# Convolved tiles of the Mamba layer made in half-product pairs ahead of the scans, and two products' rows loaded in place

## The chip, the cores and the metric

The kernel runs on one core of one Trainium2 chip. The metric is device time in microseconds (us) of one execution; lower is better. The median of three runs of the kernel before is 1600.65 us (1600.18 to 1603.64). A measurement of this kernel can tell a difference of about 0.2%, which is 3.2 us.

## The reference, cut to what matters

One step of a two-layer decoder on 1024 new prompt tokens and 8 x 8 sample tokens (1088 token columns in all), in float32. The first layer is a Mamba-2 layer, the second a pooling layer. Of the first layer only this matters here:

```python
zxbcdt = h @ w_in                                   # h: 1088 x 1024
z   = zxbcdt[..., :D_INNER]                         # 16 tiles of 128 channels, the gate
xbc = zxbcdt[..., D_INNER:D_INNER + CONV_DIM]       # 32 tiles: B, C (8 each), x (16)
conv = conv_b + sum(xp[:, k:k + L] * conv_w[k] for k in range(4))
xbc_act = jax.nn.silu(conv)
y, new_ssm = ssd_scan(xs, dt, A, Bm, Cm, ssm_prev)  # 8 groups, chunks of 128 tokens
gated = (y + d_skip * xs) * silu(z)                 # then an RMS norm per group
out = gated @ w_out
```

Group g has four convolved tiles, numbered (g, 0) for B, (g, 1) for C, and (g, 2), (g, 3) for x, and two gate tiles, 2g and 2g + 1. The last three columns of each convolved tile before the convolution are an output too (`ncT`).

## The kernel before, in words

Activations lie with channels on the 128 partitions and the 1088 tokens along the free axis. A float32 product is made of three matmuls per 128x128 weight block (high by high, high by low, low by high part).

**Two ways to make a projection tile.** The direct way (`mm3`, line 205) takes 8 blocks of the contraction x 3 chunks of 364, 364 and 360 columns x 3 matmuls = 72 matmuls; a chunk of 24 is called a unit. The half-product way (`fast_pair`, with `product` and `w_sums`) makes two tiles at once by seven half-size products instead of eight: 7 products x 2 chunks of 272 columns x 4 blocks x 3 = 168 matmuls. Its operands are sums of halves of the activations, which stand ready during the front stage, and sums of halves of the weights, which GpSimd makes; ScalarE and VectorE (and GpSimd for 2 of 7) split them.

**The front** (`front_pairs`, line 1470) makes eight such pairs, listed in `FRONT`: the twelve gate tiles 4 to 15 (stored to memory after their silu) and the four convolved tiles of group 0. `after` is called at named points within a pair and does the silus, the stores and the convolution (`proj_end`, line 388).

**The scans** (`scan`, line 1577, for groups 0 to 7, four parts p each) follow. Between a scan's small TensorE steps the order written out by hand puts units of a filler (`fills`, line 1517): `PACE[g][p]` = (a, b, c) says how many units come before `scan_front`, before `scan_y` and after it. The filler gives first the four direct tiles of each of groups 1 to 7 (`proj_group`, line 412), 12 units a group, then product 2 and product 6 of the output projection. In the scans the order on TensorE is pinned; a scheduler orders the other engines. `silu_burst` (line 397) does the silu of the next group's four tiles. VectorE convolves (`conv_tile`, line 356), scales and masks for the scan (lines 551 to 568), adds states (586, 702) and evacuates (593). The stream of weight tiles (`stream_next`) goes through three buffers `wr`, loaded by the SyncE queue (SP), with the adaLN weights of `ADA` between them.

**The output projection** also works by half-products: seven products, in the order 2, 6, 5, 3, 1, 4, 7. Each needs eight blocks `b` made of halves of the sixteen gated rows `gyd` (`block_steps`, line 1074): ScalarE copies the high part (line 1100) and VectorE subtracts (1101), after a sum or difference (1099) where two halves enter. For product 2 rows 0 to 7 are loaded whole into slots of their own (`load_row`, line 1647), kept, and used again for product 6; six of them are dropped then and loaded again for product 3. Line 1195 splits the output weights, line 1219 adds a product to the residual. `gate_last` (line 748) finishes the rows of group 7, which product 5 needs. Slots are 30 buffers of 1088 columns handed out in the order they came free.

## Time and profile before

| what | value |
|---|---|
| median of 3 runs | 1600.65 us |
| the profiled execution, its own time | 1602.45 us |
| its span in the profile | 1600.7 us |
| granted TensorE clock, mean over the span | 0.993 |
| front pairs | about 93 to 266 us |
| scans beside their filler | about 266 to 845 us |
| rest of the output projection, layer 2 | from 845 us |

The span is 1.75 us shorter than the execution's own time. A window's row gives its length, then the busy time of each engine in it, then the granted clock as a share, the busy share of the DMA engines and GB/s. Matmuls overlap, so their own durations add up to more than the time; the start-to-start distance, a stretch divided by its count, is what one costs. A wait's row says which engine and line sat idle, what ended the wait, the sum, the count and the longest.

### The profile page before, as it was taken

Reading aid. Unit: us, or ns where it says so; the run is one execution under the profiler, and the core shown is the slowest. Engines: PE = TensorE matmul, PEld = TensorE weight load, DVE = VectorE, ACT = ScalarE, POOL = GpSimd, SP = SyncE. Lnnn points to the kernel's source line nnn. Section 1 sums busy time; section 2 is a strip of 40 time slices with the busy share of each in tenths; the row PEclk is TensorE's granted clock in tenths of the full one; section 3 lists DMA queues with packets and bytes.
Section 4 is the critical chain, followed back from the end, with each engine's and each line's share of the span. In section 5 each row is a group of like instructions: output and inputs, shape, how many; then the busy total and the mean of one; then the engine's idle time right before and its main releaser. Section 6 shows DMA issues by size and latency. Waiting matters only on the chain.

```text
span 1600.7 us, 31079 instructions
## 1 busy us (share of the span) xinstructions
PE 1571.2 (98%) x12399; PEld 1514.0 (95%) x12399; DVE 1259.6 (79%) x2019; ACT 807.3 (50%) x1432; POOL 453.0 (28%) x484
## 2 busy tenths in 40 slices
PE   8999999999999999999999999999999999999997
PEld 6899999999999999999889999999999999999997
DVE  6975477888778878877987989788889777667886
ACT  6663344676666666566742468423333243333354
POOL 0133451212122122212020022765666530000231
PEclk9999999999999999999999999999999999999999
DMA  9422326866474655647779662233333379565773
GB/s 352 167 97 71 109 83 221 296 205 225 161 239 150 212 170 180 208 142 257 259 233 306 174 163 84 73 129 102 116 114 114 105 253 357 143 179 166 174 168 113
DMA packets 110730, 282.99 MB, mean 177 GB/s; under 512 B 18268, under 2 KB 42232, under 8 KB 110584
## 3 DMA queue, kind: packets, MB, share of 16 engines
q1 hardware_dynamic: 102520, 257.52, 47.0%
q0 software_dynamic: 5760, 19.01, 6.8%
q10 hardware_dynamic: 2304, 4.46, 0.7%
q8 instruction: 98, 1.61, 0.4%
q14 instruction: 48, 0.39, 0.1%
HBM read 214.59 MB, written 64.13 MB: 174 GB/s over the span
## 4 chain that ended last, share of the span: by engine, by line
PE 83%; issue 4%; DMA 4%; DVE 4%; ACT 2%; POOL 1%; SPq 0%; DVEq 0%; ACTq 0%; POOLq 0%
PE mm L101 29%; PE st L101 28%; PE op L101 13%; PE y L101 3%; PE S L101 2%; PE pl L101 2%; PE am L101 2%; PE tr L104 1%; PE tr L101 1%; DMA row<-gyd 1%; PE ms L101 1%; PE p L101 1%; DMA wr<-win 1%; DVE b L1101 1%; DMA acb<-acd 1%
## 5 line engine op out<-in xcount | busy, mean ns | idle before, releaser
L101 PE MATMUL op<-b,w 128*128 128x272 f32 x2688 | 347.0, 290 | 6.5 <-DVE w L1195 4.8
L101 PEld LDWEIGHTS op<-b,w 128*128 128x128 f32 x2688 | 341.1, 190 | 11.2 <-DVE w L1195 5.6
L101 PE MATMUL st<-hh,w 128*128 128x272 f32 x1408 | 273.9, 289 | 0.0
L101 PE MATMUL mm<-hh,wh 128*128 128x364 f32 x720 | 246.2, 342 | 0.0
L101 PE MATMUL mm<-hl,wh 128*128 128x364 f32 x720 | 236.4, 328 | 0.0
L101 PE MATMUL mm<-hh,wl 128*128 128x364 f32 x720 | 236.4, 328 | 0.0
L101 PEld LDWEIGHTS st<-hh,w 128*128 128x128 f32 x1408 | 223.9, 188 | 0.3 <-issue 0.3
L101 PE MATMUL st<-t,w 128*128 128x272 f32 x1584 | 205.6, 288 | 1.4 <-POOL w L195 1.4
L101 PE MATMUL st<-hl,w 128*128 128x272 f32 x704 | 202.8, 288 | 0.0
L101 PEld LDWEIGHTS st<-t,w 128*128 128x128 f32 x1584 | 201.1, 188 | 1.6 <-POOL w L195 1.6
L101 PEld LDWEIGHTS mm<-hh,wh 128*128 128x128 f32 x720 | 135.4, 188 | 13.5 <-issue 9.7
L193 ACT ACTIVATE w<-wr 128x512 fp32r<-128x512 f32 x88 | 55.6, 632 | 169.5 <-PE st L101 137.6
L101 PEld LDWEIGHTS mm<-hl,wh 128*128 128x128 f32 x720 | 135.4, 188 | 0.7
L101 PEld LDWEIGHTS mm<-hh,wl 128*128 128x128 f32 x720 | 135.3, 188 | 0.0
L101 PEld LDWEIGHTS st<-hl,w 128*128 128x128 f32 x704 | 132.6, 188 | 0.0
L585 POOL TENSOR_TENSOR hd<-h,cd 128x256 f32<-128x256 f32 x56 | 70.7, 1262 | 131.1 <-DVE h L586 52.4
L369 POOL COPY ncv<-raw 128x3 f32<-128x3 f32 x32 | 18.1, 564 | 287.3 <-ACT raw L439 275.7
L364 DVE SCALAR_TENSOR_TENSOR raw<-raw,vec,raw 128x1112 f32<-128x1112 f32 x64 | 90.2, 1409 | 9.8 <-ACT raw L362 9.4
L195 POOL TENSOR_TENSOR w<-wr,w 128x512 fp32r<-128x512 f32 x44 | 79.9, 1816 | 46.2 <-ACT w L193 45.9
L1219 DVE SCALAR_TENSOR_TENSOR x<-op,gat,x 128x272 f32<-128x272 f32 (+1 forms) x160 | 72.8, 477 | 25.5 <-PE op L101 23.0
L957 DVE TENSOR_TENSOR u<-st,u 128x272 f32<-128x272 f32 (+1 forms) x158 | 61.2, 408 | 38.8 <-PE st L101 36.8
L195 DVE TENSOR_TENSOR w<-sw,w 128x512 fp32r<-128x512 f32 x66 | 65.9, 998 | 26.3 <-ACT w L193 26.2
(277 smaller groups left out, 3205.1 us busy)
## 6 DMA issues: line engine op xcount, KB each, us to landing
wr<-win SPq DMA_DIRECT2D x48, 512.0 KB, 4.2
acb<-acd SPq DMA_DIRECT2D x32, 512.0 KB, 4.5
wr<-pin SPq DMA_DIRECT2D x32, 512.0 KB, 3.5
wr<-pout SPq DMA_DIRECT2D x28, 512.0 KB, 5.3
wr<-wout SPq DMA_DIRECT2D x20, 512.0 KB, 5.3
wr<-pout POOLq DMA_DIRECT2D x20, 512.0 KB, 5.8
row<-gyd SPq DMA_DIRECT2D x18, 544.0 KB, 7.8
x<-xT SPq DMA_DIRECT2D x16, 544.0 KB, 7.6
```

What stands on the lines that cost most here:

```text
L101: return self.pin(self.build.nc.tensor.matmul(*a, **k))
L104: return self.pin(self.build.nc.tensor.transpose(*a, **k))
L193: self.nc.scalar.activation(hi, src, AF.Copy)
L195: eng.tensor_tensor(out=lo, in0=src, in1=hi.bitcast(F32), op=ALU.subtract)
L364: nc.vector.scalar_tensor_tensor(out=acc[:, :n], in0=raw[:, k:k + n], scalar=w[k], in1=acc[:, :n], op0=ALU.mult, op1=ALU.add)
L369: nc.gpsimd.tensor_copy(ncv[:, 0:1, :], raw[:, 1024:1027].unsqueeze(1))
L585: nc.gpsimd.tensor_tensor(out=hd, in0=h, in1=cd[:, :, cc].unsqueeze(2).to_broadcast([P, 4, 64]), op=ALU.mult)
L957: nc.vector.tensor_tensor(out=out, in0=x, in1=y, op=ALU.add)
L1101: nc.vector.tensor_tensor(out=t[:, HALF:], in0=s, in1=t[:, :HALF].bitcast(F32), op=ALU.subtract)
L1219: ins = nc.vector.scalar_tensor_tensor(out=x[e][:, a:a + pn], in0=ps[:, :pn], scalar=g, in1=x[e][:, a:a + pn], op0=ALU.mult, op1=ALU.add)
```

## The change: what it does, and the diff

Eight convolved tiles, `MOVED`: (1, 1) to (7, 1) and (7, 2), are made in the front. The front has twelve pairs: each moved tile with one gate tile, the four tiles of group 0 in two pairs, and two pairs of gate tiles. A moved tile is convolved, gets its silu and is stored to memory (`xbd`); the filler loads it where it would have made it. The filler has 9 units for each of groups 1 to 6, and `PACE` is cut to match. The three columns for `ncT` are stored by tile in the front and by run of kept tiles in the scans. For products 2 and 6 of the output projection a new `row_blocks` loads the rows (the first half for 2, the whole for 6) straight into the block's own buffer and splits there; rows 0 to 7 are not kept, and all eight are loaded for product 3.

```diff
-PACE = (((0, 1, 2), (0, 1, 2), (0, 1, 2), (0, 1, 2)),) * 6 + (((0, 1, 2), (0, 1, 2), (0, 3, 5), (0, 0, 4)), ((0, 1, 1), (0, 1, 2), (0, 1, 0), (0, 1, 1)))
+PACE = (((0, 1, 1), (0, 1, 1), (0, 1, 1), (0, 1, 2)),) * 6 + (((0, 2, 2), (0, 2, 2), (0, 1, 2), (0, 1, 2)), ((0, 1, 1), (0, 1, 2), (0, 1, 0), (0, 1, 1)))
-FRONT = (("z", 2), ("z", 3), ("z", 4), ("z", 5), ("b", 0), ("z", 6), ("x", 0), ("z", 7))
+MOVED = tuple((g, 1) for g in range(1, 8)) + ((7, 2),)
+FRONT = ((4, 5), ((1, 1), 6), ((2, 1), 7), ((3, 1), 8), ((0, 0), (0, 1)), ((4, 1), 9), ((5, 1), 10), ((0, 2), (0, 3)), ((6, 1), 11), ((7, 1), 12), ((7, 2), 13),
+         (14, 15))
...
     def proj_end(self, G, ii, raw, ahead=False):
         dst = self.slots.get("xbc")
         self.conv_tile(G["ti"][ii], raw, dst, G["ncv"][:, ii])
+        g, nt = G["g"], self.io["ncT"][G["g"]]
         if ahead:
             self.nc.scalar.activation(dst, dst, AF.Silu)
+            self.nc.sync.dma_start(nt[:, ii], G["ncv"][:, ii])
+            if (g, ii) in MOVED:
+                self.nc.sync.dma_start(self.xbd[g, ii], dst)
+                self.slots.free(dst)
+                return
...
         for ii in range(4):
+            if (G["g"], ii) in MOVED:
+                dst = self.slots.get("xbc")
+                nc.sync.dma_start(dst, self.xbd[G["g"], ii])
+                G["out"].append(dst)
+                continue
             w = self.stream_next()
...
+    def row_blocks(self, m, lag):
+
+        nc, sl = self.nc, self.slots
+        out, raw = [], []
+        self.blocks[m] = out
+        while len(out) < 8:
+            k = len(raw)
+            if k < 8 and (sl.a[self.reserve:] or sl.b):
+                t = sl.get("b", F32R)
+                raw.append(t)
+                nc.sync.dma_start(t[:, HALF * (m == 2):].bitcast(F32), self.gyd[k][:, :HALF * (1 + (m == 6))])
+            if k >= min(len(out) + lag, 8):
+                t = raw[len(out)]
+                hi, x = t[:, :HALF], t[:, HALF:].bitcast(F32)
+                if m == 6:
+                    s = self.stage(len(out))
+                    nc.vector.tensor_tensor(out=s, in0=hi.bitcast(F32), in1=x, op=ALU.add)
+                    x = s
+                nc.scalar.activation(hi, x, AF.Copy)
+                nc.vector.tensor_tensor(out=t[:, HALF:], in0=x, in1=hi.bitcast(F32), op=ALU.subtract)
+                out.append(t)
             yield
...
         first = []
         for n, pair in enumerate(FRONT):
             outs, ends = [], []
             for i in pair:
                 if isinstance(i, tuple):
                     G = self.proj_open(i[0])
...
-        yield from itertools.islice(pr, 9)
+        yield from itertools.islice(pr, 9 - 3 * len([i for i in MOVED if i[0] == 7]))
...
-        blk = self.block_steps(2, self.rows, False, 3, self.load_row)
+        blk = self.row_blocks(2, 3)
...
-        yield from self.out_units(2, self.block_steps(6, self.rows, drop=6))
+        yield from self.out_units(2, self.row_blocks(6, 2))
```

## Rows read from the trace of the kernel before

**Rows 1.** The page: span, and busy time of each engine (share, instructions).

```profile
span 1600.7 us, 31079 instructions
PE 1571.2 (98%) x12399; PEld 1514.0 (95%) x12399; DVE 1259.6 (79%) x2019; ACT 807.3 (50%) x1432; POOL 453.0 (28%) x484
```

**Rows 2.** The chain that ended last: start, length, what, matmuls.

```profile
69.63 22.17 PE mm L101 x132
...
154.61 111.62 PE st L101 x891
...
1026.29 295.02 PE st L101 x2352
1321.31 95.62 PE mm L101 x576
```

**Rows 3.** Busy time by window: front pairs, group 0's period, group 3's period.

```profile
154.61:266.22 111.61, 111.61 (x892) 111.61 (x892) 70.78 (x125) 44.69 (x70) 43.44 (x43) 1.00 0.31 105
...
285.20:356.45 71.25, 70.40 (x574) 65.96 (x576) 56.69 (x83) 47.16 (x96) 13.99 (x25) 1.00 0.77 254
...
517.78:588.64 70.86, 70.86 (x587) 66.31 (x588) 57.32 (x79) 46.88 (x94) 14.27 (x25) 1.00 0.58 192
```

**Rows 4.** Waits of PE, first 110.43 to 266.22 us, then all of 266 to 740 us.

```profile
PE st L101 <- POOL w L195: 1.4, 1, 1.4
...
PE am L101 <- DMA wr<-adaG: 0.9, 1, 0.9
```

**Rows 5.** VectorE groups of a convolved tile, 517.78 to 588.64 us (four tiles).

```profile
L364 DVE SCALAR_TENSOR_TENSOR raw<-raw,vec,raw 128x1112 f32<-128x1112 f32 x8 | 11.2, 1401 | 0.8 <-ACT raw L362 0.8
...
L365 DVE SCALAR_TENSOR_TENSOR xbc<-raw,vec,raw 128x1024 f32<-128x1024 f32 x4 | 5.1, 1276 | 0.0
L159 DVE TENSOR_TENSOR wl<-wr,wh 128x1024 fp32r<-128x1024 f32 x4 | 4.9, 1223 | 1.3 <-ACT wh L158 1.3
...
L367 DVE SCALAR_TENSOR_TENSOR xbc<-raw,vec,raw 128x64 f32<-128x64 f32 x4 | 1.5, 367 | 0.0
```

**Rows 6.** Waits in the SP queue: 95 to 266 us, then 266 to 740 us.

```profile
SPq L450 <- ACT z L814: 45.5, 10, 11.9
...
SPq L525 <- ACT cd L566: 91.5, 25, 11.0
```

**Rows 7.** Transfers issued from 517.78 to 588.64 us: count, size, median us to landing.

```profile
acb<-acd SPq DMA_DIRECT2D x4, 512.0 KB, 5.3
...
z<-zsd SPq DMA_DIRECT2D x2, 544.0 KB, 7.1
```

**Rows 8.** Busy time by window, scans of groups 6 and 7 and what follows.

```profile
700.00:860.00 160.00, 152.59 (x1303) 142.07 (x1301) 131.74 (x220) 93.47 (x191) 27.77 (x35) 0.99 0.74 246
...
760.00:820.00 60.00, 54.97 (x508) 50.01 (x507) 57.02 (x103) 39.71 (x85) 8.80 (x10) 0.97 0.84 282
800.00:820.00 20.00, 16.37 (x149) 13.94 (x148) 18.73 (x33) 10.85 (x27) 6.00 (x4) 0.91 0.95 330
840.00:860.00 20.00, 17.93 (x145) 17.70 (x143) 11.48 (x23) 4.86 (x8) 2.04 (x3) 1.00 1.03 332
860.00:880.00 20.00, 18.87 (x130) 18.87 (x131) 18.12 (x35) 7.50 (x10) 0.87 (x1) 0.83 0.82 284
```

**Rows 9.** Waits of PE from 740 to 862 us.

```profile
PE op L101 <- DVE w L1195: 3.2, 1, 3.2
PE tr L104 <- DVE h L702: 2.5, 1, 2.5
```

**Rows 10.** VectorE around product 5's blocks and weights, in order of time.

```profile
842.29 2.62 DVE L1101 TENSOR_TENSOR b<-xbc,b 128x544 fp32r<-128x544 f32 x4
...
859.22 0.72 DVE L1099 TENSOR_TENSOR bs<-row,row 128x544 f32<-128x544 f32 x1 [6.37 <-DMA row<-gyd]
859.86 1.22 DVE L1195 TENSOR_TENSOR w<-wr,w 128x1024 fp32r<-128x1024 f32 x1
```

**Rows 11.** The chain from 825 to 845 us: last units of the scans.

```profile
831.78 3.67 PE ms L101 x16
835.45 3.05 PE op L101 x24
```

More of the change, by code (lines that the diff above doesn't have):

```diff
@@ L1072, in op_begin, with block_steps @@
         self.nc.vector.tensor_scalar(self.ngat, self.gat[l][:, :, 8], -1.0, None, op0=ALU.mult)
-    def block_steps(self, m, rows, alt=False, lag=0, load=None, drop=0, ahead=0):
+    def block_steps(self, m, rows, alt=False, load=None):
         nc, sl = self.nc, self.slots
@@ L1086, in block_steps @@
             yield
-        for i in range(lag):
-            load(i)
-            yield
         for k in range(8):
-            if load and k + lag + ahead < 8:
-                load(k + lag + ahead)
+            if load and k < 6:
+                load(k + 2)
             while not (sl.a[self.reserve:] or sl.b) or any(rows[k + 8 * o[0]] is None for o in opnds):
@@ L1301, in run @@
         items += [(io["win"][i], 8) for i in (4, 5, 10, 11)]
-        items += [(io["win"][6 * g + {"b": 0, "x": 2, "z": 4}[kind] + i], 0) for kind, g in FRONT for i in range(2)]
-        todo = [(3 * t, [(io["win"][6 * (1 + t // 4) + t % 4], 8)]) for t in range(28)]
-        todo += [(LEAD + 12 * g + (1, 4, 7, 10)[p] - 0.5, self.ada_items(a)) for (g, p), a in self.ada_plan.items()]
+        items += [(io["win"][6 * i[0] + i[1] if isinstance(i, tuple) else 6 * (i // 2) + 4 + i % 2], 0) for pair in FRONT for i in pair]
+        left = [(g, ii) for g in range(1, 8) for ii in range(4) if (g, ii) not in MOVED]
+        todo = [(3 * t, [(io["win"][6 * g + ii], 8)]) for t, (g, ii) in enumerate(left)]
+        done = lambda g, p: LEAD + sum(sum(PACE[i // 4][i % 4]) for i in range(4 * g + p)) + sum(PACE[g][p][:2])
+        todo += [(done(g, p) - 0.5, self.ada_items(a)) for (g, p), a in self.ada_plan.items()]
         for _, its in sorted(todo, key=lambda t: t[0]):
@@ new lines, in front_pairs @@
+        first = []
+        for n, pair in enumerate(FRONT):
+            outs, ends = [], []
+            for i in pair:
+                if isinstance(i, tuple):
+                    G = self.proj_open(i[0])
+                    if i[0] == 0:
+                        G["out"] = first
+                    t = self.proj_begin(G, i[1])
+                    outs.append((t, 3, t[:, 1027:1115].rearrange("p (b w) -> p b w", w=11)[:, :, 3:11]))
+                    ends.append(G)
+                else:
+                    t = sl.get("z")
+                    outs.append((t, 0, None))
+                    ends.append(None)
+            def after(x):
+                for i, at in enumerate((("B21", "B22"), ("z01", "z11"))):
+                    if x in at and not ends[i]:
+                        a = HALF * at.index(x)
+                        self.z_chunk(outs[i][0], outs[i][0][:, a:a + HALF], a, HALF)
+                    if x == ("B22", "T4")[i] and not ends[i]:
+                        self.gate_store(pair[i], outs[i][0])
+                    elif x == "B22" and ends[i]:
+                        self.proj_end(ends[i], pair[i][1], outs[i][0], True)
@@ L1514, in front_pairs @@
         self.scans = [SimpleNamespace(g=g, h=[None], M={}, acb={}) for g in range(8)]
-        self.scans[0].T = G["out"]
+        self.scans[0].T = first
     def fills(self):
@@ L1598, in scan @@
             self.units(fill, b)
-            if p == 3 and g < 6:
-                self.silu_burst(after.T)
+            if p == 3 and after:
+                self.silu_burst(after)
             self.scan_y(s, p, self.sample_y if p == 3 else None)
@@ L1630, in scan @@
             if p == 3 and after:
-                if g == 6:
-                    self.units(fill, c - 3)
-                    self.silu_burst(after.T[3:])
                 self.scan_front(after, 0)
@@ L1638, in scan @@
                     self.gate_rows(s)
-                self.units(fill, c - 1 if g < 6 else 2)
+                self.units(fill, c - 1)
             else:
@@ L1697, in load @@
                 self.load_row(k)
-        self.out_product(5, self.block_steps(3, rows, load=load, ahead=2))
+        self.out_product(5, self.block_steps(3, rows, load=load))
         self.out_product(3, self.block_steps(1, rows, True))
```

45 lines of the change are left out of this document (13 added, 32 removed).

## The prediction

> **What bounds the kernel now.** I read the page first: TensorE is busy for 98% of the span, and no other engine is above 79% [rows 1]. Matmuls overlap, so a high share alone proves little; the chain of waits comes next, and there long runs of matmuls follow one another with nothing between [rows 2]. So what counts is how many matmuls there are and how far apart they start, and then where TensorE waits. In the table of waits there is one in the front pairs (1.4 us, for a weight difference that GpSimd makes) and one in the scans up to 740 us (0.9 us, for an adaLN weight load in group 0) [rows 4]. In the steady scans TensorE is never idle, and VectorE is at 57.32 of 70.86 us, 81% [rows 3]. The stretch after that is different: from 700 to 860 us TensorE loses 160.00 - 152.59 = 7.4 us, most of it from 760 to 820 us, where VectorE is busy 57.02 of 60 us, 95% [rows 8]. Two waits stand out there, 3.2 us for output weights and 2.5 us for a sample state, both with VectorE [rows 9], and after each the granted clock drops: 0.91 and 0.83 of the windows at 800 and 860 us [rows 8], which is part of the time at 1.2 instead of 2.4 GHz.
>
> **The front gains.** A matmul of a pair starts every 111.62 / 891 = 125.3 ns; the pairs of layer 2 agree, 295.02 / 2352 = 125.4 ns. A direct one starts every 22.17 / 132 = 168.0 ns, in layer 2 every 95.62 / 576 = 166.0 ns [rows 2]. A pair costs 168 x 125.3 = 21.05 us, two direct tiles 2 x 72 x 167 = 24.05 us: 3.0 us less per pair (2.9 to 3.1 with either direct spacing). Sixteen tiles a front becomes twenty-four: four more pairs, 84.2 us, and eight direct tiles less, 96.2 us. Term 1: **-12.0 us** (-11.4 to -12.6), if nothing waits. A weighing of this term: the Trainium skill, "TensorE: Matmul & The Clock Gate", section "Back-to-back issue gap", gives for a matmul by itself the columns divided by 2.4 GHz plus 2.5 ns. That would be 115.8 and 154.2 ns here, and an estimate from it gains 2.7 us a pair and 10.7 us in all; the trace's spacings are longer, and I stay with them.
>
> **What feeds the front pairs.** Each of eight pairs now carries one convolution. By the rows of four tiles [rows 5], one costs VectorE 2 x 1.40 + 1.28 + 0.37 = 4.4 us. The old front has VectorE at 70.78 of 111.61 us with four convolutions, GpSimd at 43.44, ScalarE at 44.69 [rows 3]: 13.3 us of VectorE in each 21.05 us pair, 0.75 of a convolution included. One whole convolution a pair makes 14.5 us. So TensorE covers it, at 69%; without that cover a convolution would cost its 4.4 us. On SP a moved tile adds a state load, a store of three columns and a store of the tile, which waits for its silu; behind it stand the weight loads of the next pair. The same place already holds gate stores that wait up to 11.9 us for their silu [rows 6], and TensorE waited only the 1.4 us. I take 0 (0 to 1.4 per added pair, 5.6 in all); nothing here can go below 0.
>
> **The scans get less cover.** A period of a group, 70.86 us [rows 3], loses three units, 12.0 us, and becomes 58.8 us. VectorE loses one convolution and one weight split, 4.4 + 1.2 = 5.6 us by single durations [rows 5] (they overlap a little, so about 5.3 of busy time): 57.3 - 5.3 = 52.0 us of 58.8, 88%. ScalarE has the same loss of about 5 from 46.88: 41.9 us, 71%. Reading back a moved tile is one transfer of 544 KB, 7.1 us to landing for its like [rows 7]; it is issued at least one tile, some 12 us, before its scan begins, so it is hidden. The transposed copies and the masks of part p must be ready one unit sooner than before. The loads `acb` sit in one buffer, 5.3 us to landing [rows 7], and the SP queue waited 91.5 us in 25 times for ScalarE to give that buffer back [rows 6]; whatever stands behind, weights and moved tiles, waits with it.
>
> What these tighter scans cost TensorE no row shows. Bounds: 0, as at 81% [rows 4]; and what 760 to 820 us lost at 95%, 5.0 us of idleness and 0.09 x 20 = 1.8 us of clock, 6.8 of 60 us or 11% [rows 8], which would be 6.7 us a group. Below 0 is excluded, since these scans have no wait to lose but 0.9 us. The work is that of the 81% row, and the nearest crowding in it is group 0, whose transfers at 0.77 of the DMA engines gave one wait of 0.9 us [rows 3, 4]; with the same bytes in 58.8 us, group 3's 0.58 becomes 0.70. I take one such wait in each of six groups. Term 2: **+5.4 us** (0 to 40).
>
> **Groups 6 and 7.** Here two tiles go, 24.0 us of TensorE, counted in term 1. VectorE from 700 to 860 us has 131.74 us [rows 8] and loses 2 x 5.3: 121.1 us, which at the best sustained share of 95% needs 127.5 us. TensorE needs 160 - 7.4 - 1.8 - 24.0 = 126.8 us. The two are level, so the idleness of before (7.4 + 1.8 = 9.2 us) can shrink to 0.7, but the reason for it, VectorE at 95%, is not gone. In-place rows cost the engines nothing: the copy, the subtraction and the sum for each block are those of before. They cost transfers: eight half rows and two whole rows more, 8 x 272 + 2 x 544 KB = 3.3 MB, beside what moves at 246 GB/s with the DMA engines 0.74 busy [rows 8]. I take no change, 0 (-8.5 to +10, the latter 3.3 MB at the 332 GB/s of the fullest window).
>
> **The start of product 5.** The 3.2 us wait [rows 9] comes from VectorE: in its queue a sum of rows for product 3 waits 6.37 us for a row's landing, ahead of the weight split that TensorE needs [rows 10]. With the clock it costs 2.1 + 1.1 us of idleness and 0.17 x 20 = 3.4 us, 6.6 in all [rows 8]. Rows no longer held free slots, so these loads may come sooner; that speaks for a gain. Against it: the filler ends two units sooner, so after group 7's norm (831.78 + 3.67 us) only one unit of 3.05 us and a state product of some 1 us [rows 11] cover the blocks made from its rows, which were done at 842.29 + 2.62 = 844.9 us [rows 10]. Product 5 would ask for the first of them near 840.7 and be done with a chunk near 842.2, so a new wait of up to 2.8 us. Ends -6.6 and +2.8; neither row is nearer, so I take the middle. Term 3: **-2.0 us**.
>
> **Sum.** -12.0 + 5.4 + 0 - 2.0 = -8.6 us. The profiled execution took 1602.45 us, 1.75 more than its span and 1.8 more than the median, so it would become 1593.85, and the median 1600.65 - 8.6 = **1592.0 us**.
>
> **Rivals.**
> - The scans hold with no wait, and the late row goes: -12.0 - 6.6 = 1582 us, with groups 6 and 7 freed as well 1573.5. For it: not one wait for VectorE up to 740 us [rows 4]. Against it: 88% is new.
> - Given back: transfers of rows, 10 us on the path between 700 and 860 us, eat the front's gain, 1600.65 - 12.0 + 10 = 1598.7; or 2.0 us a group do, 1600.65. For it: 1.03 of the DMA engines at 840 us [rows 8].
> - Slower: the backlog of VectorE at the end of part 2 and in part 3 of each scan, where the sample steps and the gate's scaling meet the convolution. If the next step on TensorE waits as it does for a sample state between 800 and 820 us, 2.5 us and then 1.8 us of clock [rows 8, 9], six groups lose 26 us: 1600.65 - 12.0 + 26 = 1614.7. It decides from 12.0 / 6 = 2.0 us a group. For it: VectorE fills that stretch; against: the same stretch of each period has no wait of TensorE now [rows 4]. The rule that fits is in the Trainium skill, "TensorE: Matmul & The Clock Gate", section "HAM oscillation — how this bites in real kernels": gaps between bursts of matmuls put the engine back to the lower clock, at every gap anew. The trace agrees: 0.91 and 0.83 of the clock behind the two long waits [rows 8, 9].
> - The pairs do not gain: fed too slowly they cost the 24.05 us of two direct tiles, 1600.65 + 3. Eight old pairs speak against it.
>
> **How the numbers follow.** My forecast (some waits in the scans, 1585 to 1597) has 0.58, no waits 0.15, given back 0.12, slower 0.14, no gain in the pairs 0.01. Faster by over 0.2% is below 1597.4: 0.58 + 0.15 = 0.73. Within 0.2%: 0.13. Slower: 0.14. The range takes in the first rival down to 1577 and the second up to 1604; left out are the slower rival and the extreme of the first, under 0.2.
>
> **What would show it.** In the changed profile: twelve stretches of 168 half-product matmuls at 125 ns and an end of the front near 350 us; a period of group 1 to 5 near 59 us with VectorE near 88%; the rows of TensorE's waits inside the scans, few and under 1 us each; the granted clock at 1.00 until group 6; the wait before line 1195 gone or smaller, and one for a block at the start of product 5. A period of 61 us or more, or clock drops inside groups 1 to 5, would make the forecast wrong; so would pairs over 22 us.

## The result, and the profile after

The changed kernel takes **1622.07 us** (median of 4 runs, 1621.53 to 1626.24) where the kernel before, on the same chip, takes 1601.61: a ratio of **1.0132 [1.0112, 1.0153]**. The forecast was 1592.0 with a range up to 1604. The profiled execution took 1621.86 us.

The page and the chain of waits of the changed kernel, for [rows 1] and [rows 2]; lines in the file moved by 2 near the matmul helper (L103) and by some 35 in the later half.

```profile
span 1620.0 us, 31607 instructions
PE 1568.6 (97%) x12495; PEld 1508.3 (93%) x12495; DVE 1307.7 (81%) x2095; ACT 803.4 (50%) x1426; POOL 491.8 (30%) x508
```

```profile
153.32 185.69 PE st L103 x1482
```

TensorE is busy for 2.6 us less than before in a span that is 19.3 us longer: it waits. The front's stretch is exactly what was forecast, 185.69 / 1482 = 125.3 ns a matmul, with nothing in between. So the loss is behind it. Windows of the changed kernel (length; busy PE, weight load, VectorE, ScalarE, GpSimd; granted clock, DMA share, GB/s): the front, then the periods of groups 0, 1, 2 and 4, for [rows 3].

```profile
153.32:339.01 185.69, 185.69 (x1485) 185.69 (x1484) 147.64 (x222) 77.09 (x117) 98.48 (x97) 1.00 0.29 94
362.80:434.20 71.40, 61.20 (x503) 55.61 (x502) 54.25 (x81) 45.58 (x97) 10.88 (x21) 0.93 0.82 275
434.20:496.10 61.90, 60.84 (x535) 55.28 (x533) 51.75 (x77) 42.60 (x89) 10.95 (x21) 1.00 0.69 227
496.10:560.60 64.50, 61.08 (x515) 55.86 (x514) 52.72 (x76) 41.97 (x88) 12.65 (x21) 0.97 0.63 205
621.40:681.80 60.40, 59.43 (x514) 54.46 (x514) 50.51 (x74) 40.29 (x87) 10.94 (x21) 1.00 0.68 219
```

Group 0 takes 71.40 us, as long as before with three units more. Group 2 takes 64.5, group 4 60.4; 58.8 was forecast. Both lose to single waits. The four longest of TensorE's waits (total, times, longest), for [rows 4, 9]:

```profile
PE am L103 <- DMA wr<-adaG: 7.7, 1, 7.7
PE op L103 <- ACT w L1231: 7.1, 2, 6.3
PE tr L106 <- ACT xbc L412: 4.7, 3, 2.4
PE op L103 <- ACT raw L456: 3.6, 1, 3.6
```

**Group 0.** The chain of waits of the changed kernel, and below it what SP issued at that time (start, length, line):

```profile
375.86 5.25 DMA acb<-acd
...
381.14 1.06 ACT ea L575
382.20 2.35 ACT M L580 x8
...
385.75 4.58 DMA acb<-acd
```

```profile
375.86 0.39 SPq L542 DMA_DIRECT2D acb<-acd  x1
376.35 1.98 SPq L1183 DMA_DIRECT2D wpd<-wp  x2
378.43 3.54 SPq L1195 DMA_DIRECT2D wp<-wout  x4
385.75 0.38 SPq L542 DMA_DIRECT2D acb<-acd  x1
386.18 0.50 SPq L141 DMA_DIRECT2D wr<-adaG  x1
```

One buffer holds `acb`: the next load waits until ScalarE has read the last, so a load, an exponential (L575), nine activations on `M` (L580, L581) and a small one follow one another, 9.9 us a turn (375.86 to 385.75). SP stands until 385.75 for that buffer, and the second adaLN weight tile of part 1 stands behind it in its queue and is issued at 386.18. TensorE wanted it at 383.9 and got on at 391.7; 2.1 us more went to the weights behind it. With TensorE idle for 10.2 of the 71.40 us, some 2 us of the loss are left for the lower clock (an estimate: 12.1 us lost less 10.2). The Trainium skill, "DMA: Bandwidth & Descriptors", section "Anatomy of one DMA — SWDGE (gpsimd) path", has the rule in a clause: a DMA's semaphore wait happens on the issuing sequencer before dispatch. The section is on GpSimd's path, the clause on any wait; SP's rows show it here for SP's queue, with what it costs everything behind it.

**Groups 2 to 4.** The chain at the end of group 2:

```profile
536.00 8.52 DMA wp<-wout
...
545.64 1.13 DVE wl L161
546.77 1.65 DVE raw L366
...
552.07 1.12 ACT xbc L412
...
553.23 1.33 PE tr L106 x5
```

VectorE's queue holds, at the head of part 3, the sum of two output-weight tiles (`prep_step`, the preparation of output weights that runs beside the scans). It stands there until the second has landed, and the weight split, the convolution, the silu and the first transposes of the next scan all come late by as much. VectorE's waits from 434 to 690 us say how often:

```profile
DVE wp L1186 <- DMA wp<-wout: 12.7, 5, 3.1
```

The kernel before has no such wait in the same groups; there three of the group's four parts were a unit, 4 us, longer.

**Groups 6, 7 and product 5.** Here 3.6 us go to an eviction of ScalarE that stands behind the `acb` of group 6, and the chain ends with the split of product 5's first weight:

```profile
860.36 1.20 PE S L103 x16
861.55 5.04 issue
866.59 1.06 ACT w L1231
```

ScalarE takes the high part when the weight is there, then VectorE the low one. The weight comes by a transfer with an addition that GpSimd issued at 854.78 and that landed at 866.52, 11.7 us later, by the trace; the one before it had taken 5.8 us.

**Where the time went**, measured between marks that both traces have: last matmul of the front; first state matmul (`S<-xd,Bt`) of a group; first matmul of product 5; last of TensorE. All in us, of the profiled execution; the last two columns are the runs. The ratio is to runs of the kernel before made beside each version, whose medians lie between 1601.6 and 1603.3, so ratios compare better than medians.

| kernel | front ends | group 0 | groups 1 to 5 | group 6 to product 5 | rest | median | ratio to before, 95% |
|---|---|---|---|---|---|---|---|
| before | 265.7 | 71.3 | 357.1 | 137.1 | 744.9 | 1601.61 | 1 |
| after | 348.6 | 71.4 | 308.4 | 124.8 | 743.2 | 1622.07 | 1.0132 [1.0112, 1.0153] |
| vector_more | 349.4 | 72.3 | 312.2 | 127.8 | 743.2 | 1629.86 | 1.0175 [1.0154, 1.0195] |
| sums_later | 349.8 | 68.8 | 304.3 | 124.8 | 743.3 | 1616.03 | 1.0094 [1.0077, 1.0110] |
| ada_moved | 349.1 | 60.2 | 314.9 | 121.4 | 744.6 | 1616.11 | 1.0080 [1.0059, 1.0101] |
| no_prep | 349.6 | 58.2 | 299.3 | 124.7 | 744.1 | 1600.62 | 0.9991 [0.9981, 1.0001] |
| sums_later_ada_moved | 348.5 | 63.2 | 304.8 | 124.2 | 741.9 | 1608.64 | 1.0046 [1.0028, 1.0063] |
| prep_in_front | 379.7 | 59.2 | 299.0 | 126.3 | 743.8 | 1631.23 | 1.0179 [1.0158, 1.0200] |
| six_halves_front | 359.1 | 56.7 | 310.2 | 122.3 | 745.0 | 1613.62 | 1.0071 [1.0053, 1.0089] |
| front_from_third | 360.5 | 58.6 | 301.9 | 122.9 | 745.7 | 1612.53 | 1.0067 [1.0053, 1.0081] |
| rows_only | 265.2 | 71.3 | 357.1 | 142.1 | 748.8 | 1608.35 | 1.0032 [1.0019, 1.0046] |
| old_row_blocks | 350.3 | 71.9 | 313.7 | 128.8 | 746.9 | 1632.03 | 1.0185 [1.0158, 1.0211] |
| acb_in_slots | 349.7 | 71.7 | 310.4 | 123.1 | 743.9 | 1624.18 | 1.0137 [1.0121, 1.0153] |
| two_units_kept | 348.4 | 71.2 | 310.4 | 124.6 | 746.7 | 1627.86 | 1.0157 [1.0142, 1.0173] |
| tail_and_gpsimd | 348.6 | 70.9 | 309.8 | 129.7 | 748.6 | 1633.80 | 1.0192 [1.0177, 1.0208] |
| six_tiles | 339.4 | 58.1 | 299.9 | 137.8 | 745.7 | 1608.41 | 1.0038 [1.0025, 1.0052] |

The four other versions stand in the text. From before to after the front gains +82.9, groups 0 to 5 give back 48.6 of 72, groups 6 and 7 with product 5's start 12.3 of 24, the rest 1.7: +20.3 us. (The span grew by 19.3, since what follows TensorE's last matmul is 1.1 us shorter.)

### The profile page after: what moved, and what is told of

Read it like the earlier page. It is cut to its first block, busy times and chain, and to the rows that moved or that the text cites. A ratio compares the mean times of both kernels' runs of the same rounds, so it can differ in the third digit from the quotient of the medians.

```text
span 1620.0 us, 31607 instructions
## 1 busy us (share of the span) xinstructions
PE 1568.6 (97%) x12495; PEld 1508.3 (93%) x12495; DVE 1307.7 (81%) x2095; ACT 803.4 (50%) x1426; POOL 491.8 (30%) x508
## 4 chain that ended last, share of the span: by engine, by line
PE 77%; DVE 7%; DMA 7%; ACT 5%; issue 2%; POOL 1%; SPq 0%; DVEq 0%; ACTq 0%; POOLq 0%
PE st L103 32%; PE mm L103 18%; PE op L103 15%; PE y L103 3%; DMA wp<-wout 2%; PE pl L103 2%; DMA acb<-acd 2%; PE S L103 2%; PE am L103 1%; ACT M L580 1%; DMA wr<-pout 1%; PE tr L103 1%; PE ms L103 1%; DVE raw L366 1%; PE tr L106 1%
## 5 line engine op out<-in xcount | busy, mean ns | idle before, releaser
L103 PE MATMUL op<-b,w 128*128 128x272 f32 x2688 | 350.0, 292 | 15.6 <-ACT w L1231 7.1
L103 PEld LDWEIGHTS op<-b,w 128*128 128x128 f32 x2688 | 343.4, 191 | 21.3 <-ACT w L1231 7.7
L103 PE MATMUL st<-hh,w 128*128 128x272 f32 x1664 | 323.2, 289 | 0.0
L103 PEld LDWEIGHTS st<-hh,w 128*128 128x128 f32 x1664 | 265.4, 189 | 0.3 <-issue 0.3
L103 PE MATMUL st<-t,w 128*128 128x272 f32 x1872 | 242.7, 288 | 1.3 <-POOL w L197 1.3
L103 PE MATMUL st<-hl,w 128*128 128x272 f32 x832 | 240.6, 289 | 0.0
L103 PEld LDWEIGHTS st<-t,w 128*128 128x128 f32 x1872 | 237.4, 188 | 1.5 <-POOL w L197 1.5
L103 PE MATMUL mm<-hh,wh 128*128 128x364 f32 (+1 forms) x528 | 183.7, 348 | 2.1 <-ACT wh L160 2.1
L103 PE MATMUL mm<-hh,wl 128*128 128x364 f32 (+1 forms) x528 | 175.1, 332 | 0.3 <-DVE wl L161 0.3
L103 PE MATMUL mm<-hl,wh 128*128 128x364 f32 (+1 forms) x528 | 174.9, 331 | 0.0
L103 PEld LDWEIGHTS st<-hl,w 128*128 128x128 f32 x832 | 156.8, 188 | 0.0
L103 PEld LDWEIGHTS mm<-hh,wh 128*128 128x128 f32 x528 | 100.7, 191 | 14.0 <-issue 9.5
L103 PEld LDWEIGHTS mm<-hl,wh 128*128 128x128 f32 x528 | 100.7, 191 | 0.7
L103 PEld LDWEIGHTS mm<-hh,wl 128*128 128x128 f32 x528 | 100.4, 190 | 0.8 <-DVE wl L161 0.8
L580 ACT ACTIVATE M<-acb,tka 128x128 f32<-128x128 f32 x256 | 81.1, 389 | 24.6 <-PE y L103 13.1
L974 DVE TENSOR_TENSOR u<-st,u 128x272 f32<-128x272 f32 x174 | 67.6, 411 | 31.6 <-PE st L103 29.8
```

The source lines that it names most:

```text
L103: return self.pin(self.build.nc.tensor.matmul(*a, **k))
L580: nc.scalar.activation(M[:, r, t], acb[:, r, t], AF.Relu, bias=self.tka[cc][:, col + r:col + r + 1], scale=-1.0)
L974: nc.vector.tensor_tensor(out=out, in0=x, in1=y, op=ALU.add)
```

## The experiments

T is the theory that moved units were the cover of transfers, which come late through SP's queue, and of sums that stand in VectorE's queue for a landing; V, that VectorE's work bounds the scans.

### Is it VectorE's work, or its order?

**vector_more**, in `scan_decay` of groups 0 to 5, one pass over `M` that changes nothing:

```diff
+        if s.g < 6:
+            nc.vector.tensor_tensor(out=M, in0=M, in1=self.ones[:, 0:1].unsqueeze(1).to_broadcast([P, 4, 256]), op=ALU.mult)
```

> The changed kernel with one more VectorE pass of 128x1024 (about 1.2 us) in each part of groups 0 to 5, a multiplication by one. Theory V: each group is 4 x 1.2 = 4.8 us longer, six of them 29 us: about 1651 us. Theory T: VectorE has some 7 us to spare in a group, so a group gets 0 to 1.5 us longer: 1622 to 1631 us.

Groups 1 to 5 grew by 312.2 - 308.4 = 3.8 us, 0.8 a group, though VectorE's busy time grew by 4.4 us in each. V falls for them.

**sums_later**: the sums behind the group's last convolution in VectorE's queue.

```diff
-            self.prep_step((g, p))
+            with self.tc.issue_after(self.last_conv.ins):
+                self.prep_step((g, p))
```

> The changed kernel with VectorE's sums and differences of the prepared output weights queued behind the newest convolution instead of ahead of it. The work is the same, only the place in VectorE's queue differs. Theory T: VectorE no longer stands for a landing ahead of the convolution, so the waits for the silu at the ends of groups 2, 3 and 4 (about 2.4, 1.6 and 1.1 us, and 1.7 us of clock) go: about 1616 us. Theory V: no change, 1620 to 1624 us.

A window of group 3 of this kernel, and its longest wait of TensorE from 364 to 845 us:

```profile
557.60:617.00 59.40, 59.09 (x514) 54.37 (x514) 53.01 (x76) 41.92 (x88) 10.76 (x21) 1.00 0.68 231
```

```profile
PE mm L103 <- DVE wl L161: 8.4, 1, 8.4
```

With the same work, VectorE at 53.01 of 59.40 us (89%) leaves TensorE 0.3 us idle: the share that the prediction feared is harmless, the order was not. Groups 2 to 4 go from 64.5, 60.8, 60.4 to 59.3, 59.4, 59.5 us. In group 0, where four half sums stand in a row, the wait only changes its place.

### Is it the preparation?

**ada_moved**: one adaLN group from group 0 to group 4.

```diff
-ADA = tuple((g, p) for g in range(7) for p in ((0, 1, 2) if g == 0 else (0, 2, 3) if g == 1 else (0, 2, 3) if g == 5 else (0,) if g == 6 else (0, 2)))
+ADA = tuple((g, p) for g in range(7) for p in ((0, 2) if g == 0 else (0, 2, 3) if g == 1 else (0, 2, 3) if g in (4, 5) else (0,) if g == 6 else (0, 2)))
```

> The changed kernel with one adaLN block (two weight loads of 512 KB) taken from part 1 of group 0 to part 3 of group 4. Theory T (in the shorter scans TensorE waits for transfers that come late through the one SP queue and through the loop of the single acb buffer): the 7.7 us wait for an adaLN weight in group 0 and the time at the lower clock behind it go, group 0's period falls from 71.4 to about 62 us, the median from 1622 to about 1611 us. Theory V (VectorE at 88% is the bound of the scans): group 0 stays within 2 us of 71.4, the median within 2 us of 1622.

Group 0 falls from 71.4 to 60.2 us, and with it the longest wait. More than half of that comes back later (groups 1 to 5: +6.5, of which group 4, where the adaLN work went, +5.2), so the time is 1616 and not T's 1611.

**no_prep** leaves the preparation of output weights out of the scans; its place in memory is filled from other data in the front, so products 2 and 6 use other weights.

```diff
     def prep_step(self, key):
+        return
```

> The changed kernel without the preparation of the output weights in the scans: their loads, VectorE and ScalarE work and stores are left out there, and other data is stored in their place in the front. Theory T: group 0 falls to 60 to 63 us, groups 2 to 4 lose their waits and all come to 60.5: about 1605 us. Theory V: each group gains what VectorE loses, 13 us in group 0 and 1.3 to 2.6 in groups 1, 2 to 4: about 1601 us. This run tells what the preparation costs in all, the next one which of its parts.

A window of group 2 of this kernel:

```profile
543.60:602.90 59.30, 59.20 (x514) 54.48 (x514) 50.23 (x72) 40.82 (x86) 11.94 (x21) 1.00 0.59 196
```

TensorE has 0.1 us of idleness. Groups 0 to 5 take 357.5 us, 70.9 less than before: the scans hold the removed units almost whole, and 22.3 us of the 23.4 that they lost in the changed kernel are the preparation's. Group 6 to product 5 takes 124.7 us, as in the changed kernel, so that loss is another. The time is V's forecast (about 1601) and not T's (about 1605), but group by group neither fits: group 0 fell by 13.2 us (V 13, T 8 to 11), group 2 by 5.2 (V 1.3 to 2.6), and groups 2 to 4 came to 59.3 (T 60.5). It is vector_more that speaks against V.

This run also tells more of group 0. SP's issues there:

```profile
372.30 0.37 SPq L542 DMA_DIRECT2D acb<-acd  x1
372.77 0.46 SPq L141 DMA_DIRECT2D wr<-adaG  x1
```

The turns of `acb` are as long as in the changed kernel (10.5, 10.5 and 9.5 us), yet TensorE has no wait in group 0. The adaLN tile that came late there goes out here behind the third `acb` load, as in the kernel before; in the changed kernel two stores and four loads of the preparation follow the third, and the tile goes out behind the fourth. So a turn alone costs nothing: the loss needs the preparation in the queue as well. Whether the place in the queue or the transfers themselves make the difference was not separated in group 0: the DMA engines are 0.85 busy from 375 to 385 us of the changed kernel, and 0.46 from 370 to 380 us here.

**sums_later_ada_moved** has both edits.

> The changed kernel with both edits at once that alone gave 5 to 6 us each: the weight sums put behind the convolution, and one adaLN group moved from group 0 to group 4. If the two heal different waits (group 0's adaLN load behind acb; the silu behind the sums in groups 2 to 4), the gains add: periods of 60 to 62 in all groups, 9 to 12 us less than the changed kernel, 1610 to 1613 by the ratio (some 1608 beside a before of 1601). If they heal one and the same shortage, that of transfers behind the SP queue, the time is 1614 to 1618, no better than either alone, and one group holds a wait of 5 us or more.

It came out 13.4 us below the changed kernel (6 runs, 1607.25 to 1615.95), where the two alone gave 6.0 each: two different waits, whose gains add. The periods of groups 0, 1 and 4 (63.2, 62.9 and 62.5 us) stayed above the 60 to 62 expected.

### Can the front carry the preparation?

**prep_in_front**: sixteen halves in front pairs 1 to 7, none in the scans.

```diff
-PREP = {None: 4, (0, 0): 2, (0, 1): 2, (0, 2): 1, (0, 3): 1, (1, 3): 1, (2, 3): 2, (3, 3): 2, (4, 3): 1}
+PREP = {**{(n, x): k for n in range(1, 5) for x, k in (("B11", 2), ("T1", 1))}, **{(n, x): 1 for n in (5, 6) for x in ("B11", "T1")}}
...
+                if 0 < n < 8 and x in ("B11", "T1"):
+                    self.prep_step((n, x))
```

> The changed kernel with the whole preparation of output weights done in front pairs 1 to 7 and none of it beside the scans (same work, other place). Theory T (the moved units were the cover of the preparation's transfers and of the sums that stand for their landings): the front has room (VectorE some 17 of 21 us a pair) and its spacing stays at 125 to 126 ns, end of front within 1 us of 349; the scans are those of the run without any preparation: periods 58.2, 60.7, 59.3, 59.3, 59.3, 60.7, 60.8; time within 3 us of that run, 1598 to 1603. If the preparation costs by its mere work (bytes, VectorE) wherever it is, the front pairs grow to 22 us and more and the time stays at 1612 or above.

The scans did as expected, 358.2 us for groups 0 to 5. The front did not: 31 us longer. Its VectorE, 105 to 300 us:

```profile
DVE wp L1186 <- DMA wp<-wout: 35.6, 9, 7.0
```

The same fault as in the scans, in another place: nine sums stood for landings, 4.0 us each.

**six_halves_front** (sums_later_ada_moved with six halves in the front, each sum half a pair after its load, each store half a pair after its sum):

```diff
+                if 0 < n < 8 and x in ("z10", "T4"):
+                    self.prep_front(n, x)
```

> sums_later_ada_moved (1608.6 us) with six of the sixteen half preparations in front pairs 1 to 6, one a pair, each sum half a pair after its load and each store half a pair after its sum. By queue order (no sum stands for a landing, no store for a sum) the front stays at 348.6 to 350 and groups 0 and 1 give 2 to 6 us more (periods 59 to 61 instead of 63.2 and 62.9): 1603 to 1607. By mere work, at 31 us for sixteen halves, the front grows by 6/16 of that, 11.6 us: 360 and a time of 1615 or above.

The front grew by 10.5 us: 2.3 ahead of its first pair, 6.4 in the third (30.24 us instead of 23.81), 1.6 in the sixth, 0.1 in the first; the others with a half in them kept their 21.05. The sum is close to the 11.6 us of the reading by work, but work would be spread over the pairs, and it is not; the time, 1613.6, lies between the two readings, and groups 0 to 5 gave only 1.1 us (366.9 after 368.0). A sum half a pair behind its load still stands, 17.9 / 6 = 3.0 us (VectorE's waits, 105 to 345 us):

```profile
DVE wp L1181 <- DMA wp<-wout: 17.9, 6, 4.8
```

**front_from_third**: ten halves, loaded from the end of the third pair on, six left in groups 1 to 4.

```diff
+PREP = {(1, 3): 1, (2, 3): 2, (3, 3): 2, (4, 3): 1}
+PREP_FRONT = {2: 1, 3: 2, 4: 2, 5: 2, 6: 2, 7: 1}
```

> The changed kernel with ten of sixteen half preparations in the front, loaded from the end of the third pair on (sums from the fourth), each sum half a pair behind its load; the other six beside groups 1 to 4 with their sums behind the convolution. By place (the third pair is the tight one): the front stays within 2 us of 348.6, groups 0 and 1 take 58 to 61 us, groups 2 to 5 59 to 61; the start of product 5 at 846 to 850, time 1600 to 1605, 17 to 22 us less than the changed kernel with all its work done. By work (1.75 us a half): front 364 to 368 and time above 1615.

Neither number was met: the front is 11.9 us longer, 7.9 of it in one pair (28.99 us) with two convolutions. Waits of VectorE and GpSimd in this front (105 to 345 us), then of TensorE (140 to 360 us):

```profile
DVE wp L1182 <- DMA wp<-wout: 14.7, 6, 4.0
```

```profile
POOL sw L929 <- DMA wr<-win: 10.1, 7, 3.4
```

```profile
PE st L104 <- POOL raw L387: 4.9, 2, 4.1
```

The sums wait as before, and now GpSimd waits 10.1 us for the front's own weights, 3.0 in the changed kernel. So place alone was not it either; with ten halves as with six, SP's queue delivers neither the sums' tiles nor, now, the front's weights in time. The DMA engines are not full there (0.47 to 0.64 busy from 248 to 268 us), and SP stands up to 6.4 us for the stores of the preparation. That this is what delays the loads is likely, not shown: a front whose loads have a queue of their own wasn't tried.

### Groups 6, 7 and product 5

**rows_only**: the kernel before with the in-place rows alone.

```diff
-        blk = self.block_steps(2, self.rows, False, 3, self.load_row)
+        blk = self.row_blocks(2, 3)
...
-        yield from self.out_units(2, self.block_steps(6, self.rows, drop=6))
+        yield from self.out_units(2, self.row_blocks(6, 2))
```

> The kernel before, with the in-place row blocks of products 2 and 6 alone (front, moved tiles and pace as before). The prediction gave this part -2.0 us (ends -6.6 and +2.8) at the start of product 5, and 0 (-8.5 to +10) in groups 6 and 7. If the blocks or their transfers (3.3 MB more) are themselves a cause of the slowdown, this kernel is 3 to 10 us slower than the kernel before and a wait for a block or for a weight of 3 us or more stands between 700 and 860 us. If the part is harmless, as the trace after suggests (its waits there are for weights and for an eviction, none for a block), the time stays within 3 us of the kernel before, 1598 to 1604, and the wait at the start of product 5 for a row is gone or exchanged for one of like length for weights.

The ratio is 1.0032 [1.0019, 1.0046], 5.6 us by the medians. TensorE's waits from 708 to 900 us:

```profile
PE op L101 <- DVE w L1218: 3.8, 2, 3.4
PE y L101 <- DVE h L586: 3.0, 1, 3.0
PE tr L104 <- DVE h L702: 2.0, 1, 2.0
```

None over 0.8 us is for a block. The time is that of the first reading (3 to 10 us slower), with a wait of 3 us or more for a weight. That wait is about as long as before (3.4, before 3.2), and one for a state grew from 1.0 to 3.0. VectorE ahead of the split:

```profile
864.02 0.72 DVE L1099 TENSOR_TENSOR bs<-row,row 128x544 f32<-128x544 f32 x1 [6.53 <-DMA row<-gyd]
864.66 1.22 DVE L1218 TENSOR_TENSOR w<-wr,w 128x1024 fp32r<-128x1024 f32 x1
```

The late row stands ahead of the split just as the prediction read it ([rows 10]; 6.53 us, before 6.37), and TensorE goes on at 865.94. In-place rows alone do not bring that row sooner.

**old_row_blocks**, the changed kernel with rows as before (and two units fewer in `PACE`'s entry for group 6):

```diff
-        blk = self.row_blocks(2, 3)
+        blk = self.block_steps(2, self.rows, False, 3, self.load_row)
...
-((0, 2, 2), (0, 2, 2), (0, 1, 2), (0, 1, 2))
+((0, 1, 1), (0, 1, 1), (0, 2, 2), (0, 1, 3))
```

> The changed kernel without its in-place rows: products 2, 6 and 3 take their rows as before, with two units fewer in group 6's pace because the rows hold slots. If the in-place blocks cost 5 us by themselves, as in the kernel before with that part alone, this is 4 to 6 us faster than the changed kernel: 1616 to 1618; the wait at the start of product 5 is again behind VectorE. If their cost there came from the old pace and is none in the new one, the time is 1620 to 1625.

10 us slower, a miss for both readings: group 6 to product 5 takes 4.0 more, groups 1 to 5 5.3 more. So beside the new pace the in-place rows are not what costs. But the run changes the pace of group 6 too, and groups 1 to 5, where no row is loaded yet, lost more than the rest: why is not known, and how much is the rows' own stays open.

**acb_in_slots**: the `acb` of groups 6 and 7 double buffered.

```diff
+        if s.g >= 6 and (s.g, p) != (6, 0):
+            s.acbt[p] = self.slots.get("acb")
```

> The changed kernel, with the broadcast loads acb of groups 6 and 7 (all but the first) put into free slots, so that one can land while the other is still read. If the 3.9 us wait of TensorE at 770 us (an eviction behind the chain of acb landing, exponentials and masks in ScalarE's queue) comes from the single buffer, it shrinks below 1 us, the half clock behind it (3.4 us at half) goes, and the start of product 5 moves from 867.5 to 861 to 864: 4 to 6 us faster than the changed kernel, 1616 to 1618. If the wait comes from VectorE or from the silu burst ahead of the scan, it stays and the time is within 1.5 us of 1622.

The wait at 770 us fell from 3.6 to 1.1 us, as T had it, and the place gained 1.7; a wait of 3.4 us for adaLN's `mp` at 754 us took the rest. The time did not gain: the 4 to 6 us did not come.

**two_units_kept** (`PACE`'s entry for group 6) and, on top of it, **tail_and_gpsimd**:

```diff
-((0, 2, 2), (0, 2, 2), (0, 1, 2), (0, 1, 2))
+((0, 2, 2), (0, 2, 2), (0, 1, 1), (0, 1, 1))
```

```diff
-                    nc.vector.tensor_tensor(out=s, in0=hi.bitcast(F32), in1=x, op=ALU.add)
+                    nc.gpsimd.tensor_tensor(out=s, in0=hi.bitcast(F32), in1=x, op=ALU.add)
```

> The changed kernel, with two units of filler fewer in parts 2 and 3 of group 6, so that they are left for the end of the scans, ahead of product 5. If product 5 waits (6.6 + 1.9 us, then 10.2 us at half clock) for output weights whose load and split take their own time from the moment that the scans let them start, the two units (some 6 us) cover them: the wait falls to 3 us or less and the start of product 5 moves by 3 to 6 us, to 861.5 to 864.5; time 1616 to 1619, less what part 2 and 3 of group 6 lose by waits. If the weights are late because the queues ahead of them are, the units only move the wait: start of product 5 within 1.5 us of 867.5, and time within 2 us of 1622.

> The changed kernel with the two units kept for the end (as in two_units_kept) and the eight row sums of product 6 (0.72 us each, 5.7 us in all) on GpSimd instead of VectorE. If VectorE's work is what bounds groups 6 and 7, the waits for it at 796 and 828 us (3.0 and 3.0 us, with two half-clock stretches of 3.4 and 6.8 us behind them) shrink to 1 us each or go, and the start of product 5 moves from 868.8 to 859 to 863: time 1618 to 1622. If single late steps bound it and not the sum of its work, the waits stay and the time is 1625 to 1630.

With two units kept, the wait at product 5 is gone, but group 6 to product 5 takes as long as before that edit (124.6 us) and the time is worse than both readings: two other waits stand in parts 2 and 3 of the scans. Waits of TensorE from 700 to 880 us:

```profile
PE tr L106 <- DVE h L719: 2.9, 1, 2.9
PE tr L106 <- DVE xd L568: 2.8, 1, 2.8
```

With the sums on GpSimd (to 900 us), and GpSimd's group for them from 790 to 850 us:

```profile
PE tr L106 <- DVE xd L568: 5.2, 1, 5.2
PE tr L106 <- DVE h L719: 2.9, 1, 2.9
```

```profile
L1138 POOL TENSOR_TENSOR raw<-b 128x544 f32<-128x544 f32 x7 | 10.7, 1526 | 21.2 <-DMA b<-gyd 10.3 <-DVE b L1141 6.3 <-issue 2.7
```

The time, 1633.8, is above both readings. The run meant to take 5.7 us of sums from VectorE, but from group 6 to product 5 its busy time fell by 0.7 us only (109.3 to 108.6). Its product on `M`, first with two units kept, then with the sums on GpSimd:

```profile
L584 DVE TENSOR_TENSOR M<-M,cb 128x1024 f32<-128x1024 f32 x7 | 9.1, 1301 | 1.6 <-ACT M L581 1.5
L584 DVE TENSOR_TENSOR M<-M,cb 128x1024 f32<-128x1024 f32 x7 | 11.5, 1645 | 0.2 <-ACT M L581 0.2
```

The longest, 2384 ns, ran beside a sum on GpSimd; the same step took 1218 without. A sum also takes GpSimd 1526 ns, VectorE 719, so the sums came later. So this run settles nothing on VectorE: neither its total nor the order of its queue is cleared.

### Is there a version that beats both?

**front_prep_old_rows** (prep_in_front with old_row_blocks), 1635.80 us, 1.0203:

> Both edits: preparation in the front and rows as before. If they add, 1594 to 1598, faster than the kernel before by 5 us: group 0 to 5 as in the run without preparation. If the rows' part depends on the pace and gives nothing here, 1599 to 1603.

**front_prep_six** (the same with six tiles and the old pace; the last tile of group 7 goes without its silu), 1628.98 us, 1.0164, front to 359.6, groups 0 to 5 358.1:

> Preparation in the front, six moved tiles (groups 1 to 6, one each; 11 front pairs), and group 7's tiles, the pace of groups 6 and 7 and the rows as in the kernel before. Theory T: front 328 to 330, periods of groups 0 to 5 of 58 to 61 (sum 357 to 361 against 428.5 before), groups 6 and 7 and the start of product 5 as before (71.9 and 65.2): 5 to 8 us faster than the kernel before, ratio 0.995 to 0.997, 1593 to 1597. If groups 0 to 5 do not hold 12 us each, the time is 1600 or above.

**later_moved_tail_gpsimd** (sums_later_ada_moved with the last two edits), 1619.06 us, 1.0096, group 6 to product 5 128.2:

> sums_later_ada_moved (1608.6 us) with the tail and the GpSimd sums. If the gains of the scans and of the end are independent, the wait of 5.9 + 1.9 us and the 6.8 us at half clock at the start of product 5 (some 11 us) go without new ones: 1598 to 1602. If the end is bound by VectorE or by single steps, 1606 to 1612.

**all_mended** (that with six halves in the front), 1622.33 us, 1.0123:

> All of it: sums later, one adaLN group moved, six halves of the preparation in the front, two units kept for the end, row sums of product 6 on GpSimd. If every part gives what it is meant to: 1594 to 1599, level with the kernel before or faster by up to 0.4%. If the front or the end give back: 1604 or above.

None gave what the parts promised: what is freed in one place is waited for in the next. **six_tiles**, the last, takes the loss out where it was known, with front_from_third's preparation, and the scans' order, `PACE`'s entry and the rows of groups 6 and 7 as before:

```diff
-MOVED = tuple((g, 1) for g in range(1, 8)) + ((7, 2),)
+MOVED = tuple((g, 1) for g in range(1, 7))
...
-((0, 2, 2), (0, 2, 2), (0, 1, 2), (0, 1, 2))
+((0, 1, 2), (0, 1, 2), (0, 3, 5), (0, 0, 4))
```

> The same with six moved tiles (one each of groups 1 to 6, 11 front pairs), and group 7, the pace of groups 6 and 7, and all rows as in the kernel before. If what the changed kernel lost beyond the preparation lies in groups 6 and 7 and product 5: front 328 to 331, groups 0 to 5 together 357 to 362 (428.5 before), groups 6 and 7 as before (71.9 and 65.2), the start of product 5 at 838 to 841 against 845.3, time 1594 to 1598: faster than the kernel before by 0.2 to 0.4%. If the late groups lose as much from the front's or the scans' new timing, 1601 or above.

A window of its groups 0 to 5:

```profile
353.60:711.60 358.00, 356.79 (x3102) 327.94 (x3102) 305.81 (x440) 249.22 (x516) 66.68 (x126) 1.00 0.64 212
```

The scans are as T has it: 358.0 us, TensorE idle for 1.2 of them, full clock, VectorE at 85%. Groups 6 and 7 are as before (137.8). The front ends at 339.4 instead of 329, and these 10 us are more than the 7 that were to be won: 1608.41 us, 1.0038 [1.0025, 1.0052]. It is the nearest of all that move tiles and compute everything, but none of those beat the kernel before.

## Why the prediction was wrong, point by point

Of the 30.1 us between forecast and median, groups 0 to 5 make 18.0 (forecast -72.0 + 5.4, measured -48.6) and group 6 to product 5 11.7 (forecast -24.0, measured -12.3). The front was 1.3 us better than forecast and the rest 0.3 worse (forecast -2.0, measured -1.7); 1.0 is the kernel before on this chip, and 0.4 is between the profiled execution and the median. Term 3 is counted to the rest: the wait it was to shorten stood at 861 us, behind product 5's first matmul at 845.3.

- **The front (Term 1), right.** 125.3 ns in 1482 matmuls and an end 82.9 us later, against 84.2. Feeding cost nothing, as said, but with less to spare than reckoned: VectorE is busy for 147.64 of 185.69 us, 80% and not 69%. One convolution takes 6.0 us of it there (2 x 1.46 + 2.04 + 1.03), not the 4.4 of the scans' rows. Its pass of 128x1024 in that window:

```profile
L367 DVE SCALAR_TENSOR_TENSOR xbc<-raw,vec,raw 128x1024 f32<-128x1024 f32 x11 | 22.4, 2035 | 0.0
```

Of the front's twelve such passes the nine that ran beside GpSimd's work on weights took 2.3 us, the other three 1.28. The estimate from the Trainium skill, "TensorE: Matmul & The Clock Gate", section "Back-to-back issue gap", would have had the pairs at 115.8 ns; the new pairs side with the old rows.
- **Less cover (Term 2, +5.4), the step that failed.** The loss in groups 0 to 5 is 23.4 us: 12.1 in group 0, 11.3 in the others. "I take one such wait in each of six groups" priced it by the length of one wait in a period that still had its cover (0.9 us, [rows 4]); that wait for `adaG` became 7.7 us when the group lost three units, its transfer going out behind one more `acb` turn of 9.9 us in SP's queue, and the price had no lower clock in it. [Rows 6] had shown the turns (SP waited 91.5 us in 25 times for that buffer) and the prediction named them, yet set no price on them. And the preparation of output weights, which runs beside the scans, does not appear in the prediction at all: without it (no_prep) 22.3 of the 23.4 us are gone, with the turns as long as they were. In the longer periods before it cost next to nothing (TensorE idle for 0.9 us of group 0's, [rows 3]), so it is the preparation and the lost cover together. For groups 2 to 4 sums_later shows which part: the sums' place in VectorE's queue. For group 0 it stays open which part, as said there.
- **VectorE at 88% was the wrong measure.** The changed kernel has 84% in group 4; 89% in sums_later holds with 0.3 us idle. The share that was watched cost next to nothing (0.8 us a group in vector_more); a queue that stood for landings, 12.7 us in five times in groups 1 to 4, did.
- **Reading a moved tile back, right.** No wait of TensorE, VectorE or ScalarE is for one; GpSimd has one, of 2.2 us.
- **Groups 6 and 7 (0) and product 5 (Term 3, -2.0).** Up to product 5 the two tiles were to give 24.0 us and gave 12.3, the second step that failed: "no change" in groups 6 and 7. TensorE's idleness there rose from 5.3 us (708.2 to 845.3 in the kernel before) to 13.4 (742.6 to 867.5 in the changed one), the largest part a new wait of 6.3 us for product 5's first weight. The kept units remove it, the double `acb` cuts the one at 770 us, and each time others follow. What orders these single steps is not settled: no run took work from VectorE there, and none gave the weights' additions another queue. Term 3 has its number (-1.7 in the rest), but not by its reason: rows_only shows that in-place rows do not bring the row sooner. In the changed kernel the longest wait for a row is 1.6 us, but product 5 starts late there; with the kept units, where it does not wait, one row is waited for 5.4 us again. So the number is luck as far as the runs show. The new wait of up to 2.8 us for blocks did not come (0.8 at most); by the prediction's own rows that end was 3.9, since 835.45 + 3.05 and some 1 us give 839.5 and not 840.7.
- **The rivals.** "Slower" had the sign and the break-even, 2.0 us a group (measured 3.9), by a backlog of VectorE that vector_more refutes for groups 1 to 5. Its half-clock part came: behind the long waits the granted clock is 0.93 of group 0's window and 0.97 of group 2's. The Trainium skill, "TensorE: Matmul & The Clock Gate", section "HAM oscillation — how this bites in real kernels", says that gaps between bursts of matmuls put the engine back to the lower clock; these two did.
- **What would show it.** "A period of 61 us or more, or clock drops inside groups 1 to 5": both came: 61.9 us in group 1, 64.5 us and a clock of 0.97 in group 2.

## What to carry to other kernels

Work moved out from beside a scan was also the cover of that scan's transfers: list each transfer that is issued there, with its turn (issue, landing, release of the buffer) and what stands in front of it in its queue, and compare that turn with the new period. A sum of loaded data in an in-order queue must come late enough behind its load that it never stands; here a share of 89% busy was no danger, a 3 us stand ahead of the next convolution was. And price the background work that the change does not touch. Price a step by rows of the place it moves to: the convolution's rows came from the scans, and in the front, beside GpSimd's work, it took 6.0 us instead of 4.4.

## What the runs showed of the hardware that was not expected

- The same 128x544 sum takes 719 ns on VectorE and 1526 ns on GpSimd, and it does not free VectorE by as much: eight of them moved took 0.7 us from its busy time, not 5.7.
- The 128x1024 pass of a convolution on VectorE takes 1.28 us by itself and 2.3 us beside GpSimd's sums and splits of weights (three and nine passes in the front of the changed kernel).
- Two 256 KB loads with a sum behind them, half a pair (some 10 us) later in program order, still stood 3.0 us on average in the front. A load landed 3.6 to 4.8 us after SP issued it, so what counted was not the distance in the program, but SP's lateness in issuing it.
- Group 0's window, with the longest wait, has a granted clock of 0.93, so part of it ran at 1.2 GHz instead of 2.4; group 2's, with a wait of 2.4 us, 0.97; group 4's, whose longest wait was 0.9 us, 1.00.
